# Storing and broadcasting the forgetting gates' sums from GpSimd's DMA queue instead of SyncE's

## The chip, the cores and the metric

The kernel runs on one core of one Trainium2 chip. The metric is the device time of one execution in microseconds (us), as the median of the runs; lower is better. The core's engines are named as in the profile: PE is TensorE, the matrix engine, with PEld for its weight loads; DVE is VectorE; ACT is ScalarE; POOL is GpSimd; SP is SyncE, which only issues transfers here. DMAs are issued from an engine's queue and carried out by 16 transfer engines.

## The reference

A trunk of two layers over 256 tokens of width 1024, in float32. Layer 0 mixes by forgetting attention (12 heads of 64), layer 1 by block-sparse attention with ALiBi; each also has 4 heads of attention into 256 memory tokens, and each is followed by a SwiGLU network. What the change touches is the forgetting gate of layer 0:

```
log_f = log_sigmoid(f_logit + b_fgate)          # per token and head
F = cumsum(log_f, axis=-1)                      # (heads, tokens)
s = q @ k.T * scale + F[..., :, None] - F[..., None, :]
p = softmax(where(causal, s, NEG));  out = p @ v
```

So every head needs F along the queries, one value per row of the scores, and F along the keys, one value per column, the same in all rows.

## The kernel before, in words

All matrix products are made in split precision: each float32 operand is cut into a high part (ACT, a copy that rounds, `hi`, line 204) and a low part (DVE, a subtraction, `lo`, line 205), and three products are summed in PSUM. Weights are laid out on the host as one stream of units of up to 2048 elements per partition (8 KB on each of 128 partitions, 1 MB in all). `fetch` (line 178) loads one unit into one of four `raw` buffers, from SP's queue; `split` (line 195) cuts half a unit into `hi` and `lo`, of which there are seven buffers each. A unit's fetch must wait until the unit four before it is split. `weights` (line 211) runs the splitting five halves ahead of PE's use, and `split` runs the fetching three units ahead of that.

`mixer` (line 430) makes one layer's attention. It first makes the values and, in layer 0, the gate logits; from these `lf` (lines 450 to 460) is log_f with tokens on the partitions. Then come three groups of queries and keys (`qk_ps`), of two head pairs each. Ahead of the second group, in layer 0, stands `memory_heads` (line 507): `mem_kv` (line 312) makes the keys and values of the memory (`mk`, `mv`), with the inverse root of the memory's mean square `rs_mem`, taken by POOL (line 245) and spread over the columns by PE and ACT as `rsb_mem` (line 257); then the memory queries `qm` are made, scaled and split into `xqm` (lines 351 to 353), and the keys into `mks` (lines 358 to 361). In these splits ACT makes the high parts, and POOL and DVE one low part each.

The attention of a pair of heads is a generator (`attend`, line 363) that is advanced by `step` between the products, so that its parts stand between other work. Among these generators is `gate_sums` (line 472). It makes the running sums F on PE as a product with a triangular matrix, with heads on 12 partitions; DVE copies them to `fr` (line 478); a DMA stores `fr` to the DRAM tile `fd` (line 479), and three DMAs read `fd` back, four heads each, broadcast to all 128 partitions of `fk` (line 482). F along the queries, `fq`, is made on PE and ACT directly. `bias` (line 489) joins `fk`, `fq` and the causal mask on DVE, head pair by head pair, and overwrites `fk`; the scores read the result (line 385).

The order of PE's and SP's instructions is that of the program's text (`manual_schedule`, line 713). The order on DVE, ACT and POOL is chosen by the compiler's scheduler, which may move an instruction ahead of others when its operands allow. Each engine then runs its own list strictly in order: an instruction that waits holds all that stand behind it, and the same is true of the DMAs in an engine's queue.

Of the kernel before, what the change touches and what calls it, by code (L numbers as in the profile page):

```python
# [28 lines left out]
P = 128  # L29
D = 1024  # L30
S = 256
NT = S // P
KD = D // P
H = 12
# [18 lines left out]
GATE_PARTS = 3  # L53
# [74 lines left out]
def trunk(ctx: ExitStack, tc: tile.TileContext, plan, stream, x, gains, norm_final, b_fgate, square, out):  # L128
    nc = tc.nc
# [27 lines left out]
    def bank(name):  # L157
        return Bank(pp.tile([P, 512], F32, tag="bank", name=name))
# [135 lines left out]
    fd = dp.tile([H, S], F32, name="fd")  # L294
    fk = cp.tile([P, H, S], F32, name="fk")
# [134 lines left out]
    def mixer(i, xs, rs):  # L430
# [41 lines left out]
        def gate_sums():  # L472
            yield
            fb = bank("F_ps")
            fb.mm(fb.t[:H, 0:S], lf[:, 0], prefix)
            fb.mm(fb.t[:H, P:S], lf[:, 1], prefix[:, 0:P], stop=True)
            fr = ap.tile([P, 2, S], F32, tag="work", name="fr", bufs=WORK_BUFS)[:H, 0]
            nc.vector.tensor_copy(fr, fb.t[:H, :S])
            nc.sync.dma_start(fd, fr)
            for g in range(GATE_PARTS):  # L480
                hs = slice(g * (H // GATE_PARTS), (g + 1) * (H // GATE_PARTS))
                nc.sync.dma_start(fk[:, hs], fd[hs].unsqueeze(0).to_broadcast([P, H // GATE_PARTS, S]))
            gb = bank("Fq_ps")
            for t in range(NT):
                for u in range(t + 1):
                    gb.mm(gb.t[:, t * H:(t + 1) * H], prefix[:, (t - u) * P:(t - u + 1) * P], lf[:, u], stop=u == t)
            nc.scalar.activation(fq.rearrange("p t h -> p (t h)"), gb.t[:, :NT * H], AF.Copy)
# [43 lines left out]
        for g in range(3):  # L531
            if g == MEM_AT[i]:
                memory_heads()
            kb = [bank(f"qk_ps{i}{2 * g + a}") for a in range(2)]
            for k in range(KD):
                wh, wl = weights(U["qk", i, g][k // 4], k % 4)
                for a in range(2):
                    for s in range(2):
                        c = slice(a * P, (a + 1) * P)
                        prod(kb[a], kb[a].t[:, s * S:(s + 1) * S], (wh[:, s, c], wl[:, s, c]),  # L540
                             (xs[0][:, k, :], xs[1][:, k, :]), k == KD - 1)
                if k % 2:
                    step()
            if g == 0:
                rsb = spread(rs, f"x{i}", (DH ** -0.5, 1.0), "x")
                if i == 0:
                    active.append(gate_sums())
            for a in range(2):
                p = 2 * g + a
                qk = ap.tile([P, 2, S], F32, tag="work", name=f"qk{i}{p}", bufs=WORK_BUFS)  # L550
                nc.vector.tensor_mul(qk.rearrange("p a s -> p (a s)"), kb[a].t, rsb.rearrange("p a s -> p (a s)"))
                xq = ap.tile([P, 2, S], F32R, tag="work", name=f"xq{i}{p}", bufs=WORK_BUFS)
                xk = ap.tile([P, 2, 2 * S], F32R, tag="pair", name=f"xk{i}{p}", bufs=PAIR_BUFS)
                no_lo(xk)
                split_queries(xq, qk[:, 0])
                split_keys(xk, qk[:, 1])
                idle = a + IDLE[i][g]
                active.append(attend(f"s{i}{p}", xq, xk, vsb, 2 * p, idle, bias, hT, p))
# [203 lines left out]
```

## Time and profile before

| what | value |
|---|---|
| median of 3 runs (lowest to highest) | 628.83 us (628.81 to 631.61) |
| the profiled execution's own time | 632.32 us |
| its span, first to last instruction | 630.5 us |
| busy, share of the span: PE, PEld, DVE, ACT, POOL | 97%, 83%, 63%, 58%, 10% |
| moved by DMA | 112.27 MB, mean 178 GB/s |
| PE's share of the chain of waits that ended last | 83% |

All stretches and durations come from the profiled execution; its time lies 3.5 us above the median of the runs. Times in the rows are us from the start of the span. In a timeline a row is the start, the duration, the engine, the line of the kernel, the operation, output<-input by the program's names, and in brackets the idle time of the engine ahead of it with what ended it; a q behind an engine's name is its sequencer or queue. For a DMA the duration is that of the issue, not of the transfer. The chain of waits is followed back from the last instruction through what released each step.

### The profile page before, as it was taken

How to read it: one execution, taken by the hardware profiler on the slowest of the kernel's cores; microseconds unless marked ns; L12 is line 12 of the kernel's file. 1: busy time of each engine (PE TensorE's matmuls, PEld its weight loads, DVE VectorE, ACT ScalarE, POOL GpSimd, SP SyncE). 2: the span in 40 equal slices, each digit the busy share in tenths (PEclk: the TensorE clock that was granted, in tenths of full speed). 3: DMA queues.
4: the chain of work that ended last, by engine and by line, in shares of the span. 5: the costliest groups of instructions: out<-in, count | busy, mean ns of one | idle time of the engine just before them, and what ended most of it. 6: DMA issues, size and time to landing. Idle time of an engine off the chain costs nothing.

```text
span 630.5 us, 8923 instructions
## 1 busy us (share of the span) xinstructions
PE 611.7 (97%) x3364; PEld 525.4 (83%) x3364; DVE 400.2 (63%) x696; ACT 363.0 (58%) x648; POOL 62.3 (10%) x91
## 2 busy tenths in 40 slices
PE   7999899999999999999999999999999999999994
PEld 5999887778888888888899999877888888888884
DVE  5678899976455544457475689986654455544535
ACT  6778877666444444446376589866644444444432
POOL 2021344300000000000011032200000000000002
PEclk9999799999999999999999999999999999999999
DMA  8985822345555555555555642332455555455301
GB/s 297 385 283 177 329 72 96 144 158 200 201 194 173 176 191 201 182 174 202 193 185 199 218 147 106 133 135 94 157 189 196 193 180 169 193 200 201 134 1 67
DMA packets 17636, 112.27 MB, mean 178 GB/s; under 512 B 2221, under 2 KB 2873, under 8 KB 5433
## 3 DMA queue, kind: packets, MB, share of 16 engines
q1 hardware_dynamic: 17304, 111.49, 49.1%
q8 instruction: 26, 0.43, 0.3%
q10 hardware_dynamic: 288, 0.22, 0.1%
q14 instruction: 18, 0.14, 0.1%
HBM read 110.64 MB, written 1.06 MB: 177 GB/s over the span
## 4 chain that ended last, share of the span: by engine, by line
PE 83%; DVE 7%; ACT 5%; DMA 2%; issue 1%; POOL 0%; SPq 0%; POOLq 0%; ACTq 0%; DVEq 0%
PE gu L167 38%; PE d_acc L167 18%; PE qk_ps L167 8%; PE v_ps L167 5%; PE o_acc L167 5%; DMA raw<-in_stream 2%; DVE lo L205 2%; PE hT L628 2%; ACT hi L204 1%; PE s_s L167 1%; ACT p_s L395 1%; PE mv_ps L167 1%; PE qm_ps L167 1%; PE mk_ps L167 1%; PE s_m L167 1%
## 5 line engine op out<-in xcount | busy, mean ns | idle before, releaser
L205 DVE TENSOR_TENSOR lo<-raw,hi 128x1024 fp32r<-128x1024 f32 (+3 forms) x201 | 238.3, 1203 | 159.8 <-ACT hi L204 154.5
L204 ACT ACTIVATE hi<-raw 128x1024 fp32r<-128x1024 f32 (+3 forms) x201 | 204.8, 1037 | 165.6 <-PE gu L167 78.9
L167 PE MATMUL gu<-hi,xh_ffn 128*128 128x512 f32 x352 | 139.0, 395 | 0.0
L167 PE MATMUL gu<-lo,xh_ffn 128*128 128x512 f32 x352 | 137.3, 390 | 0.0
L167 PE MATMUL gu<-hi,xl_ffn 128*128 128x512 f32 x352 | 137.1, 390 | 0.0
L167 PE MATMUL d_acc<-hi,h 128*128 128x512 f32 x348 | 107.5, 390 | 0.0
L167 PEld LDWEIGHTS gu<-lo,xh_ffn 128*128 128x128 f32 x352 | 66.1, 188 | 13.9
L167 PEld LDWEIGHTS gu<-hi,xl_ffn 128*128 128x128 f32 x352 | 66.2, 188 | 13.2
L167 PEld LDWEIGHTS gu<-hi,xh_ffn 128*128 128x128 f32 x352 | 66.1, 188 | 13.1
L167 PEld LDWEIGHTS d_acc<-hi,h 128*128 128x128 f32 x348 | 65.2, 188 | 13.8 <-DVE h L224 0.4
L167 PE MATMUL d_acc<-lo,h 128*128 128x512 f32 x174 | 67.7, 389 | 0.0
L167 PE MATMUL qk_ps<-xh_x,hi 128*128 128x256 f32 x192 | 55.8, 291 | 0.0
L167 PE MATMUL qk_ps<-xh_x,lo 128*128 128x256 f32 x192 | 55.1, 287 | 0.0
L167 PE MATMUL qk_ps<-xl_x,hi 128*128 128x256 f32 x192 | 55.1, 287 | 0.0
L619 ACT ACTIVATE sg<-gu,rs_f 128x256 f32<-128x256 f32 x44 | 20.5, 466 | 40.0 <-PE gu L167 40.0
L167 PEld LDWEIGHTS qk_ps<-xh_x,hi 128*128 128x128 f32 x192 | 37.7, 197 | 0.8 <-issue 0.8
L167 PEld LDWEIGHTS d_acc<-lo,h 128*128 128x128 f32 x174 | 32.7, 188 | 6.7
L167 PEld LDWEIGHTS qk_ps<-xh_x,lo 128*128 128x128 f32 x192 | 37.8, 197 | 0.0
L167 PEld LDWEIGHTS qk_ps<-xl_x,hi 128*128 128x128 f32 x192 | 37.6, 196 | 0.0
L620 DVE TENSOR_TENSOR hh<-gu,sg 128x256 f32<-128x256 f32 x44 | 18.5, 421 | 27.0 <-ACT sg L619 27.0
L395 ACT ACTIVATE p_s<-p_s,nmax_s 128x128 f32<-128x128 f32 (+1 forms) x48 | 21.4, 447 | 12.9 <-DVE nmax_s L385 12.7
L303 POOL MEMSET xk<- 64x256 f32 x24 | 7.4, 310 | 206.1 <-PE d_acc L167 180.7
(158 smaller groups left out, 852.3 us busy)
## 6 DMA issues: line engine op xcount, KB each, us to landing
raw<-in_stream SPq DMA_DIRECT2D x95, 1024.0 KB, 4.8
raw<-in_stream SPq DMA_DIRECT2D x4, 768.0 KB, 4.4
raw<-in_stream SPq DMA_DIRECT2D x2, 780.0 KB, 8.6
fk<-fd SPq DMA_DIRECT2D x3, 512.0 KB, 5.2
raw<-in_stream SPq DMA_DIRECT2D x3, 390.0 KB, 6.0
h<-in_x SPq DMA_DIRECT2D x2, 512.0 KB, 7.4
raw<-in_stream SPq DMA_DIRECT2D x1, 512.0 KB, 7.3
gfin<-in_norm_final SPq DMA_DIRECT2D x1, 512.0 KB, 3.6
```

The source lines that it names most:

```text
L167: nc.tensor.matmul(o, lhsT, rhs, start=self.fresh, stop=stop, skip_group_check=True)
L204: nc.scalar.activation(hi[:, c0:c1], src[:, c0:c1], AF.Copy)
L205: nc.vector.tensor_sub(lo[:, c0:c1], src[:, c0:c1], hi[:, c0:c1].bitcast(F32))
L303: nc.gpsimd.memset(dst[HOME[1 - a], a, S:].bitcast(F32), 0.0)
L395: nc.scalar.activation(pr[:, a, c], src, AF.Exp, bias=nmax[:, a, j], scale=scale, accum_out=total[:, a, j])
L619: nc.scalar.activation(sg[:, t], b[t].t[:, :FC], AF.Silu, scale=rs[t])
L620: nc.vector.tensor_mul(hh[:, t], b[t].t[:, FC:], sg[:, t])
L628: nc.tensor.transpose(b.t[:, j * S + t * P:j * S + (t + 1) * P], hh[:, t, j * P:(j + 1) * P], ident)
```

## The change

The store of the gates' sums and the three broadcasts are issued from POOL's DMA queue; nothing else in the text is changed.

```diff
             fr = ap.tile([P, 2, S], F32, tag="work", name="fr", bufs=WORK_BUFS)[:H, 0]
             nc.vector.tensor_copy(fr, fb.t[:H, :S])
-            nc.sync.dma_start(fd, fr)
+            nc.gpsimd.dma_start(fd, fr)
             for g in range(GATE_PARTS):
                 hs = slice(g * (H // GATE_PARTS), (g + 1) * (H // GATE_PARTS))
-                nc.sync.dma_start(fk[:, hs], fd[hs].unsqueeze(0).to_broadcast([P, H // GATE_PARTS, S]))
+                nc.gpsimd.dma_start(fk[:, hs], fd[hs].unsqueeze(0).to_broadcast([P, H // GATE_PARTS, S]))
```

## Rows read from the trace of the kernel before

**Rows 1.** The page: PE's busy time, and PE's granted clock in 40 slices.

```profile
PE 611.7 (97%) x3364; PEld 525.4 (83%) x3364; DVE 400.2 (63%) x696; ACT 363.0 (58%) x648; POOL 62.3 (10%) x91
...
PEclk9999799999999999999999999999999999999999
```

**Rows 2.** PE's waits, longest in total: total us, times, longest.

```profile
PE s_m L167 <- POOL xqm L353: 2.9, 1, 2.9
```

**Rows 3.** Windows: busy us of PE, PEld, DVE, ACT, POOL; PEclk, DMA share, GB/s.

```profile
63.00:64.00 1.00, 0.00 (x0) 0.00 (x0) 0.56 (x2) 0.95 (x3) 0.22 (x1) 1.00 1.09 414
64.00:65.00 1.00, 0.00 (x0) 0.00 (x0) 0.84 (x3) 0.95 (x3) 0.69 (x1) 0.66 0.98 311
...
70.00:72.00 2.00, 2.00 (x14) 2.00 (x14) 0.31 (x2) 0.00 (x0) 0.00 (x0) 0.72 1.01 426
```

**Rows 4.** The chain of waits in order of time, from 48 to 70.

```profile
52.42 6.83 DMA raw<-in_stream
...
65.12 2.08 PE s_m L167 x8
```

**Rows 5.** ACT's timeline from 52 to 64.

```profile
52.30 0.46 ACT L342 ACTIVATE mv<-mv_ps,rs_mem 128x256 f32<-128x256 f32 x1
...
59.33 1.06 ACT L204 ACTIVATE hi<-raw 128x1024 fp32r<-128x1024 f32 x1 [2.15 <-DMA raw<-in_stream]
```

**Rows 6.** DVE's timeline from 44 to 66.

```profile
45.15 0.41 DVE L478 COPY fr<-F_ps 12x256 f32<-12x256 f32 x1
...
50.44 2.36 DVE L205 TENSOR_TENSOR lo<-raw,hi 128x1024 fp32r<-128x1024 f32 x2 [0.58 <-ACT hi L204]
...
58.28 0.68 DVE L338 TENSOR_TENSOR mk<-mk_ps,rsb_mem 128x512 f32<-128x512 f32 x1
...
60.42 1.23 DVE L205 TENSOR_TENSOR lo<-raw,hi 128x1024 fp32r<-128x1024 f32 x1 [0.86 <-ACT hi L204]
...
63.87 0.61 DVE L499 SCALAR_TENSOR_TENSOR bias<-fk,fq,sq 128x128 f32<-128x128 f32 x2
```

**Rows 7.** SP's queue, timeline from 48 to 62.6.

```profile
49.82 2.92 SPq L187 DMA_DIRECT2D raw<-in_stream  x2
52.80 0.43 SPq L479 DMA_DIRECT2D fd<-fr  x1
59.46 1.30 SPq L482 DMA_DIRECT2D fk<-fd  x3
60.85 1.83 SPq L187 DMA_DIRECT2D raw<-in_stream  x3
```

**Rows 8.** POOL's groups by shape: busy us, mean ns of one, idle before.

```profile
L494 POOL TENSOR_SCALAR fk<-sq 128x256 f32<-128x256 f32 x12 | 14.5, 1209 | 15.2 <-DVE nmax_s L385 8.0 <-issue 6.5 <-POOL xk L303 0.2
...
L303 POOL MEMSET xk<- 64x256 f32 x24 | 7.4, 310 | 206.1 <-PE d_acc L167 180.7 <-PE s_s L167 20.7 <-issue 4.1
```

**Rows 9.** POOL's timeline from 44 to 66.

```profile
45.09 0.73 POOL L361 TENSOR_TENSOR xk<-qk,xk 64x256 fp32r<-64x256 f32 x1
50.00 0.55 POOL L245 TENSOR_TENSOR rs_mem<-me_mem,minus_half 128x1 f32<-128x1 f32 x1 [4.18 <-DVE me_mem L243]
...
60.77 1.47 POOL L361 TENSOR_TENSOR mk<-mk,mk 64x256 fp32r<-64x256 f32 x1 [7.28 <-ACT mk L358]
62.51 0.71 POOL L361 TENSOR_TENSOR mk<-mk,mk 64x256 fp32r<-64x256 f32 x1 [0.26 <-ACT mk L358]
```

**Rows 10.** DMA issues by line: count, KB each, median us from issue to landing.

```profile
fk<-fd SPq DMA_DIRECT2D x3, 512.0 KB, 5.2
...
out<-o SPq DMA_DIRECT2D x1, 320.0 KB, 2.5
```

**Rows 11.** The same windows as in rows 3, earlier stretches.

```profile
48.00:50.00 2.00, 2.00 (x19) 2.00 (x18) 1.86 (x3) 2.00 (x5) 0.00 (x0) 1.00 0.00 0
50.00:52.00 2.00, 2.00 (x19) 2.00 (x18) 1.56 (x2) 2.00 (x3) 0.55 (x1) 1.00 0.51 135
...
57.00:59.00 2.00, 2.00 (x19) 2.00 (x18) 2.00 (x4) 0.18 (x1) 0.00 (x0) 1.00 0.05 21
```

## The prediction

> **What bounds the kernel now.** The page first: TensorE (PE) is busy for 97% of the span, and its granted clock is at full speed (2.4 GHz) in all slices but two near a tenth of the span [rows 1]. So the change can only matter where PE waits. The waits of PE come next: the longest one after the start-up is 2.9 us, for GpSimd's (POOL's) split of the memory queries `xqm` [rows 2]. The windows around it show what this stop costs beyond itself: PE is idle in 63 to 64, the clock is 1.00 there, 0.66 in 64 to 65 and 0.72 in 70 to 72, so it lay at its half level (1.2 GHz) from about 64.3 to 71.1 [rows 3]. PE works again from 65.12 [rows 4], so 6.0 us of its work ran at half speed, which lost some 3.0 us. At stake around this place are thus 2.9 + 3.0 = 5.9 us.
>
> The change's four transfers lie just ahead of it. The chain of waits, read back from 65.12, goes through ScalarE's (ACT's) key and query splits to a weight fetch that was issued at 52.42 and landed 6.83 us later, at 59.25 [rows 4]. I call it B, and the fetch issued before it at 49.82 I call A. ACT stood idle 2.15 us for B, because `hi` of B lies ahead of the key splits in its queue [rows 5]. The keys `mk` themselves were ready on VectorE (DVE) at 58.28 + 0.68 = 58.96 [rows 6], and ACT took them up after 59.33 + 1.06, at 60.3 to 60.4: the wait for B costs the chain 1.3 us. The landing of B is what the whole prediction turns on.
>
> **What is removed.** On SyncE's queue (SP) the store of `fd` waited behind A and B: its data `fr` were ready at 45.15 + 0.41 = 45.56 [rows 6], it was issued at 52.80, and the three broadcasts of `fk` only at 59.46, because SP stood for the landing of `fd`; three more weight fetches then followed from 60.85 [rows 7]. Four issues (0.43 + 1.30 = 1.73 us) and a wait of 6.2 us leave SP. I cost that at nothing: B is issued ahead of `fd` in either kernel, so it does not start earlier, and the fetches behind, which could start up to 8 us earlier, line up after B; the chain goes on through no other fetch up to 65.12 [rows 4], so none of those three was late. The first reader of `fk` on DVE, the bias at 63.87 [rows 6], is off the chain too.
>
> **What is added on POOL.** Four DMA issues and one wait. No row shows a DMA issued from POOL. Its price g lies between POOL's memset (0.31 us) and its costliest full-tile instruction (1.21 us) [rows 8], with more as a possibility for the upper end; I take 1.2, since descriptors for 128 rows are nearer to the full tile. POOL ends its last key split at 45.82 [rows 9], so `fd` is issued at 45.9 and handed over at 47.1. The quickest landing in the trace took 2.5 us from issue, some 2.1 of it behind the issue itself [rows 10]; the transfer engines are empty in 48 to 50 [rows 11]. So `fd` lands near 49.2. POOL waits for that (about 2 us), then issues the three broadcasts, 3 x 1.2 = 3.6 us, up to 52.8. Behind them in POOL's queue stands the square root `rs_mem`, which before ran at 50.00 for 0.55 us [rows 9]; it would end at 53.4, 2.8 us late. Who waits: ACT's `mv` at 52.30 [rows 5], which slips to 53.4, by 1.1 us. That is inside the 1.3 us by which `mk` was early, so it costs nothing as long as that cover stands.
>
> **What is moved on the transfer engines.** This is the term that I count. The broadcasts move 3 x 512 KB [rows 10]; at 426 GB/s, the rate of a full stretch [rows 3], that is 1.573 MB / 0.426 = 3.7 us. Before, they ran after B. Now their first data come at about 50.4, beside A and ahead of B's last row. In 50 to 52 the engines had a share of 0.51 [rows 11], so 0.98 us was free. If all of `fk` is served before B ends, B lands 3.7 - 1.0 = 2.7 us later. A row of `raw` is 8 KB on each partition and one of an `fk` part 4 KB; if the two queues take turns row by row, only 1.05 MB of `fk` goes ahead of A's and B's 2.1 MB, 2.5 - 1.0 = 1.5 us. I take the middle, **2.1 us**; the ends are 0 (nothing ahead of B) and 3.7 (none of it in free time). B then lands at 61.35, `hi` of B, the key splits, `xqm` and PE's restart all come 2.1 us later, and the half-clock stretch behind it is as long as before. POOL's 1.1 us on ACT hides in the longer wait.
>
> One thing about B I carry over without knowing that it recurs: in 57 to 59 the share is 0.05 [rows 11], about one of 16 engines, so a single engine finished B two microseconds after the others.
>
> The Trainium skill ("DMA: Bandwidth & Descriptors", Anatomy of one DMA) gives about 2.0 us of fixed cost to a DMA from GpSimd. By that estimate `fd` would land at 47.9, `fk` would use more of the empty stretch, and the sum would be about 630 us; no run here shows it.
>
> **Sum.** The profiled execution took 632.32 us for a span of 630.5; the median of the runs is 628.83, 3.5 lower. The difference of +2.1 us is set against the median: 628.8 + 2.1 = **630.9 us**.
>
> **Rivals.**
>
> *POOL becomes the path (slower).* If an issue from POOL takes longer than I took, `rs_mem` is what is late. It ends at 48.55 + 4g; of a delay of ACT's `mv` beyond 52.30 the first 1.3 us are hidden, the rest moves PE's restart, in place of the 2.1 and not on top of it. Over 3.1 us late is reached with g = 2.0 (`rs_mem` at 56.7). A reason for it: DVE's `lo` subtraction held a POOL split, which took 1.47 us from 60.77 beside a `lo` from 60.42 to 61.65, where the next one took 0.71 with none beside it [rows 6, 9]. The `lo` pair from 50.44 lasts 2.36 us and falls on the broadcasts [rows 6]. Held once in full and with g at 1.5, `rs_mem` ends at 48.55 + 6.0 + 2.36 = 56.9: 4.6 - 1.3 = +3.3 us, **632.1**, and up to 634 if two are held. Against it: a DMA issue need not behave like a split that reads two tiles.
>
> The Trainium skill ("SBUF — State Buffer", SBUF: two separate sides) says that a DVE operation with two SBUF inputs locks out only a GpSimd operation that reads SBUF, while one in a 2-port mode keeps GpSimd from writing descriptors. By that rule `lo` would hold the splits, as the rows show, but not the issues, and the sum would stay at 630.9; by the hold of the rows it is 632.1 or more.
>
> *The wait for B goes away (faster).* If the engine that finished B late was late through the neighbourhood of `fd`, or if the compiler's new order on ACT puts the key splits ahead of `hi` of B, the key splits start at 58.96: 1.3 us earlier, and PE restarts at 63.8. The clock was still 1.00 in the window 63 to 64 [rows 3], so the half-speed stretch and its 3.0 us could go as well: 628.8 - 4.3 = **624.5**. Against it: `fk` must then not delay B, though it is moved towards it.
>
> *Nothing is seen.* `fk` is generated late or slowly enough to run after B, and POOL stays within its 1.3 us: **628.8**.
>
> *The order is not what the text of the kernel says.* Only PE's and SP's orders are fixed by hand. If `rs_mem` is put ahead of the broadcasts on POOL, its delay vanishes and the broadcasts start at about 53.5; B is still in transit, so 1 to 2 us remain: **630**.
>
> **How the numbers follow.** My forecast (B late by contention) gets 0.47, its own range 628.8 to 632.5; 0.05 of it lies over the bound. POOL as the path 0.22, the wait for B gone 0.16, nothing seen 0.10, other order 0.05. A measurement of this kernel tells about 0.5% (3.1 us) from no change: faster 0.16; slower 0.22 + 0.05 = 0.27; within it 0.57. The range reaches from the faster rival, 624.5, to 633.2, inside the slower one; what lies beyond (half of the faster case, under half of the slower) is 0.18.
>
> **What would show it.** Right: the `fd` store on POOL before 47, `fk` issued between 49 and 53, B's landing at 61 to 62, ACT's idle time before `hi` of B near 4 us, PE's wait for `xqm` near 5 us, one half-clock stretch as before. Wrong: B landing at or before 59.3; PE's wait named for `rsb_mem` or for `mv` instead; ACT taking the key splits before `hi` of B; PE's clock at full speed throughout; or another PE wait of microseconds elsewhere, which would mean that the order of ACT, DVE or POOL changed in a way that these rows cannot show.

## The result and the profile after

The changed kernel takes **633.43 us** (median of 8 runs, 632.70 to 634.26). The kernel before, run beside it, took 630.56 (8 runs, 628.81 to 631.61; the three runs shown ahead of the prediction are among them). The ratio is 1.0051 with a 95% interval of 1.0034 to 1.0068: 2.1 to 4.3 us slower. The forecast was 630.9 in a range of 624.5 to 633.2, so the time lies 0.2 us above its upper end.

PE's first page row is the same as before but for 0.2 us, and PE's waits show one change that matters. First the page's busy times and the clock of the changed kernel, then PE's longest wait after the start-up.

```profile
PE 611.9 (97%) x3364; PEld 525.6 (83%) x3364; DVE 399.9 (63%) x696; ACT 363.6 (57%) x648; POOL 65.0 (10%) x95
...
PEclk9999799999999999999999999999999999999998
```

```profile
PE s_m L167 <- POOL xqm L353: 5.7, 1, 5.7
```

The wait of [rows 2] has grown from 2.9 to 5.7 us. PE's busy time is equal to 0.2 us, so in these two executions the change is a matter of waiting alone. POOL has four instructions more, the four issues.

POOL's timeline (as in [rows 9]) shows what these cost there.

```profile
45.66 0.76 POOL L479 DMA_DIRECT2D fd<-fr  x1
48.37 1.62 POOL L482 DMA_DIRECT2D fk<-fd  x3 [1.96 <-DMA fd<-fr]
50.01 0.59 POOL L245 TENSOR_TENSOR rs_mem<-me_mem,minus_half 128x1 f32<-128x1 f32 x1
```

A store issue takes 0.76 us and a broadcast 0.54, against the 1.2 I took. All three broadcasts are issued before `rs_mem` is due, and `rs_mem` runs at 50.01, where it ran before (50.00). POOL delays nobody.

The chain of waits of the changed kernel, from 46 to 70, is the one to set against [rows 4].

```profile
47.23 2.10 DVE lo L205 x2
49.33 0.18 issue
49.51 0.11 DVE me_mem L243
49.62 9.11 DMA raw<-in_stream
58.76 0.04 issue
58.80 1.07 ACT hi L204
59.87 0.02 issue
59.90 1.25 DVE lo L205 x2
...
62.17 0.69 DVE mk L338
...
67.65 0.04 issue
67.69 2.07 PE s_m L167 x8
```

It does not go through B any more. The fetch in it was issued at 49.62: that is **A**, which landed 9.11 us later, at 58.73. Before, the same issue landed in 4.7 us, at 54.5, as the view of DMA issues of the kernel before, cut to 49 to 51, says (count, KB, us to landing):

```profile
raw<-in_stream SPq DMA_DIRECT2D x1, 1024.0 KB, 4.7
```

So A lost 4.2 us. ACT's timeline shows who stood for it (compare [rows 5]).

```profile
53.99 0.82 ACT L342 ACTIVATE mv<-mv_ps,rs_mem 128x256 f32<-128x256 f32 x2
58.80 2.01 ACT L204 ACTIVATE hi<-raw 128x1024 fp32r<-128x1024 f32 x2 [3.99 <-DMA raw<-in_stream]
60.72 0.36 ACT L256 ACTIVATE rsb_mem<-rsb_ps_mem 128x256 f32<-128x256 f32 x1
61.29 1.06 ACT L204 ACTIVATE hi<-raw 128x1024 fp32r<-128x1024 f32 x1 [0.21 <-DMA raw<-in_stream]
62.89 0.42 ACT L358 ACTIVATE mk<-mk 64x256 fp32r<-64x256 f32 x1 [0.54 <-DVE mk L338]
```

ACT is idle 3.99 us for A and only 0.21 us for B. The broadcast scale `rsb_mem` stands behind `hi` of A in ACT's list, and `mk` needs `rsb_mem`; on DVE `mk` also stands behind the two `lo` of A (59.90 to 62.17). So `mk` was made at 62.17 instead of 58.28 [rows 6], 3.9 us late; 1.3 us of this had been slack in which ACT stood for B, and PE's restart moved by 67.69 - 65.12 = 2.6 us. B itself landed at 61.2 against 59.25, 2.0 us late.

The windows show the cause (columns as in [rows 3]; compare [rows 11]).

```profile
48.00:50.00 2.00, 2.00 (x19) 2.00 (x18) 1.65 (x3) 2.00 (x5) 1.62 (x3) 1.00 0.13 25
50.00:52.00 2.00, 2.00 (x19) 2.00 (x19) 1.76 (x2) 2.00 (x3) 0.59 (x1) 1.00 1.00 277
...
57.00:59.00 2.00, 2.00 (x19) 2.00 (x18) 0.00 (x0) 0.20 (x1) 0.00 (x0) 1.00 1.03 430
...
70.00:72.00 2.00, 2.00 (x11) 2.00 (x11) 1.92 (x4) 1.98 (x5) 0.00 (x0) 0.50 0.00 0
```

The transfer engines, empty from 57 to 59 before, are full from 50 to 66 now, and DVE does nothing from 57 to 59, where it was busy all the time before.

**Where the time stands in the whole.** The first `gu` product, which begins the SwiGLU network of layer 0, splits the span well. It starts at 134.28 in the profile of before and at 136.23 in that of after; the profiled executions took 632.32 and 634.26. What is left behind that point is 498.04 and 498.03 us. The whole difference lies ahead of the first `gu`.

These two executions differ by 1.9 us, the medians by 2.9: the profiled execution of before lies 1.8 us above its median, that of after 0.8 above its own. The mean granted clock, which is known of every run, tells more. Among this case's profiles a mean of 0.996 to 0.998 goes with no stretch at the half level, 0.993 to 0.995 with one of some 3.4 us, 0.990 to 0.992 with one of some 6.8 us; the two executions here, at 0.992 and 0.990, are both of the last kind. Of 79 further runs of the kernel before, 25 are of the first kind, with a median of 629.05 us, 49 of the second, with 630.67, and 4 of the third, with 632.03 (one, at 0.944, is left aside). Of the changed kernel's 8 runs 7 are of the third kind, with a median of 633.53, and one, 632.81, is of the second. So at like clock the changed kernel is 1.5 to 2.1 us slower, and by this estimate the rest of the 2.9 us, about 1, is that it nearly always has the longer stretch at the half level.

### The profile page after: what moved, and what is told of

It reads as the page before. It is cut to its first block, busy times and chain, and to the rows that moved or that the text cites. A ratio compares the mean times of both kernels' runs of the same rounds, so it can differ in the third digit from the quotient of the medians.

```text
span 632.5 us, 8922 instructions
## 1 busy us (share of the span) xinstructions
PE 611.9 (97%) x3364; PEld 525.6 (83%) x3364; DVE 399.9 (63%) x696; ACT 363.6 (57%) x648; POOL 65.0 (10%) x95
## 4 chain that ended last, share of the span: by engine, by line
PE 83%; DVE 7%; ACT 5%; DMA 2%; issue 1%; POOL 0%; SPq 0%; POOLq 0%; DVEq 0%; ACTq 0%
PE gu L167 38%; PE d_acc L167 18%; PE qk_ps L167 7%; PE v_ps L167 5%; PE o_acc L167 5%; DVE lo L205 2%; DMA raw<-in_stream 2%; PE hT L628 2%; ACT hi L204 1%; PE s_s L167 1%; ACT p_s L395 1%; PE mv_ps L167 1%; PE qm_ps L167 1%; PE mk_ps L167 1%; PE s_m L167 1%
## 5 line engine op out<-in xcount | busy, mean ns | idle before, releaser
L167 PE MATMUL qk_ps<-xh_x,lo 128*128 128x256 f32 x192 | 55.2, 287 | 0.0
```

The lines of the kernel that those rows point to most:

```text
L167: nc.tensor.matmul(o, lhsT, rhs, start=self.fresh, stop=stop, skip_group_check=True)
```

## The experiments

Four theories. **T1**: the broadcasts go ahead of A, and PE's wait for `xqm` is the cost. **T2**: the compiler's new order on DVE and ACT is the cost. **T3**: issuing on POOL is the cost. **T4** replaced T1 after the second set of runs: what ACT and DVE lose while they stand for A is the cost, and PE's wait is only where it shows. Intervals are for the ratio to the kernel before, run on the same chip (630.23, 630.41 and 630.60 us in the three sets).

**The store alone on POOL.**

```diff
-            nc.sync.dma_start(fd, fr)
+            nc.gpsimd.dma_start(fd, fr)
```

> The store of the gates' sums is issued by POOL, the three broadcasts stay on SP. SP's list then has the two weight fetches A and B first and the broadcasts right behind them, with the store long landed. Theory T1 (the broadcasts' 1.5 MB, put ahead of A and B on the transfer engines, delays the memory keys and so PE's restart): A lands by 54.5 and B by 59.3 as in the kernel before, PE's wait for xqm is 2.9 us or less, and the time is that of the kernel before (ratio 0.994 to 1.001). Rival T2 (the compiler's new order on ACT and DVE costs the time): this order differs from that of before too, so a loss of some microseconds is possible. Rival T3 (DMA issues on POOL are what costs): about a quarter of the loss, +0.8 us.

Measured: 629.83 us, ratio 0.9997 (0.9981 to 1.0012). In its profile A lands at 55.2 and B at 58.9. The three broadcasts are issued on SP right behind B (53.3 to 54.9), without SP standing for `fd`, and land at 60.6 to 63.1, in time for the first bias. PE's wait is 2.2 us and no stretch is at the half level. So this DMA costs nothing that is measured by being issued on POOL, and neither does it gain anything that SP no longer waits 6.2 us.

**All four on POOL, the broadcasts held back until `rsb_mem` exists** (a one-column copy from it into each part of `fk`).

```diff
+            yield from iter(lambda: len(rsb_mem), 1)
...
+                nc.gpsimd.tensor_copy(fk[:, hs.start, 0:1], rsb_mem[0][:, 0:1])
                 nc.gpsimd.dma_start(fk[:, hs], fd[hs].unsqueeze(0).to_broadcast([P, H // GATE_PARTS, S]))
```

> All four transfers on POOL as in the change, but each broadcast is held until the factors rsb_mem exist (a one-column copy of rsb_mem into fk on POOL stands ahead of each), so that its data come behind A and mostly behind B. T1: A lands as in the kernel before, PE's wait for xqm is 2 to 3.5 us, time ratio to before 0.995 to 1.002. T3 (issuing on POOL costs): the loss of the change stays, ratio 1.005. T2 (order): the lists on ACT and DVE are near those of before, so no loss either; this run tells T1 and T2 apart from T3 alone.

Measured: 631.79 us, ratio 1.0027 (1.0012 to 1.0041). A lands at 54.5, B at 57.1, and PE's wait for `xqm` is down to 1.5 us: the delay of A hangs on the broadcasts' time. But the broadcasts, issued from 58.6 on, came behind three weight fetches that SP had issued meanwhile, and landed at 68.3 to 70.8. DVE's first bias, at 63.87 before [rows 6], was late, and PE waited elsewhere. Both rows of PE's waits in this kernel:

```profile
PE qk_ps L167 <- ACT p_m L395: 1.9, 2, 1.2
PE s_m L167 <- POOL xqm L353: 1.5, 1, 1.5
```

**The kernel before, with the change's four transfers made in addition** (through a second DRAM tile, from POOL's queue).

```diff
+    fd2 = dp.tile([H, S], F32, name="fd2")
...
+            nc.gpsimd.dma_start(fd2, fr)
+            [nc.gpsimd.dma_start(fk[:, 4 * g:4 * g + 4], fd2[4 * g:4 * g + 4].unsqueeze(0).to_broadcast([P, 4, S])) for g in range(3)]
             nc.sync.dma_start(fd, fr)
```

> The kernel before, with the change's four transfers added on POOL (a store to a second DRAM tile and three broadcasts from it into fk), and the kernel's own store and broadcasts kept on SP behind them. The lists of PE, DVE and SP are those of the kernel before; ACT's differs in the place of one mv. T1: A lands 4 us late (58 to 59), PE's wait for xqm grows to 5 to 6 us, time +2.5 to +4 us against before (ratio 1.004 to 1.0065). T2 (the compiler's new order of DVE and ACT costs the time): no loss, ratio 1.000. T3: a loss, but with A landing as before.

Measured: 634.38 us, ratio 1.0071 (1.0050 to 1.0092). PE's, DVE's and SP's lists are those of the kernel before, and ACT's differs in one `mv`. Still ACT stands for A as in the changed kernel:

```profile
58.76 2.01 ACT L204 ACTIVATE hi<-raw 128x1024 fp32r<-128x1024 f32 x2 [3.70 <-DMA raw<-in_stream]
```

PE's wait is 5.4 us. T2 falls: the extra transfers suffice without the new order.

**Only the first of the three broadcasts**, in the changed kernel (the other eight heads' `fk` set to zero, so their scores lack the gates' sums along the keys). In a first try the zeros were written by POOL near the start; that moved the whole start by 1 us (PE's first wait 4.5 instead of 2.8), so its 631.40 us, ratio 1.0022 (1.0008 to 1.0036), tells little.

```diff
+    nc.gpsimd.memset(fk[:, H // GATE_PARTS:], 0.0)
...
-            for g in range(GATE_PARTS):
+            for g in range(1):
```

> The change with only the first of the three broadcasts; the part of fk for the other eight heads is filled with zeros once, on POOL near the start, so these heads lack the gates' term along the keys. A third of the bytes stands ahead of A and B, and the lists of ACT and DVE are nearly those of the change. T1: A lands about 1.4 us later than before instead of 4.2, PE's wait for xqm is 3 to 4 us, time 0 to +1 us against before (ratio 1.000 to 1.002). T2: the loss of the change stays, ratio 1.005.

With the zeros written by DVE (`nc.vector.memset`) the start is as before:

> The changed kernel with only the first of the three broadcasts; the other eight heads' fk is set to zero on DVE near the start instead of on POOL, and their scores lack the gates' sums along the keys, so it leaves a part of the computation out. T1: 0.5 MB instead of 1.5 MB goes ahead of A, so A lands a third of the way from its place in the kernel before (54.5) to that in the changed one (58.7), about 55.9; PE's wait for xqm is 3.5 to 4.2 us and the time 1 us above the kernel before, a ratio of 1.000 to 1.003. Rival (the cost is one of issuing or of the first DMA, not of bytes): A lands near 58.7 and the time is that of the changed kernel, 1.005.

Measured: 631.19 us, ratio 1.0010 (0.9995 to 1.0025). A lands at 55.7, PE's wait is 3.2 us.

```profile
55.77 2.01 ACT L204 ACTIVATE hi<-raw 128x1024 fp32r<-128x1024 f32 x2 [0.89 <-DMA raw<-in_stream]
```

A third of the bytes gives some three tenths of A's delay (1.2 of 4.2 us) and a fifth of the cost (0.0010 of 0.0051, with an interval from nothing to half). The delay goes with the bytes, not with the first DMA.

**The first memory scores one step later in PE's order**, in the kernel before, in the changed one, and with the store alone on POOL. PE then has some 54 more products to do ahead of the place where it stood.

```diff
-IDLE_MEM = (1, 1)
+IDLE_MEM = (2, 1)
```

> The kernel before, with the memory heads' scores of the first two pairs put one step (some 54 products, about 6.3 us of PE at full speed) later in PE's order. It is the partner of the next run. Every theory: PE no longer stands 2.9 us for xqm at its first memory score, so that stop and the half-speed stretch behind it go, unless the split weights that it now reaches earlier are late themselves: 624.5 to 629, a ratio of 0.991 to 0.998 to the kernel before, with A landing near 54.5 and B near 59.2 as there.

> The changed kernel with the same later step. T1 (the change costs time only because the broadcasts delay fetch A and with it xqm, for which PE stands): A still lands near 58.7 and xqm is still ready near 67.5, but PE has about 6.3 us of products ahead of its first memory score and hardly stands for it, so the distance to its partner shrinks from 3 us to under 1 us: 625 to 629.5. T1b (the late fetch A starves PE directly, whatever stands at the memory score): PE waits 1 to 3 us for the split weights of A instead, and 2 to 3 us to the partner stay. T3 (issuing four DMAs on POOL costs time elsewhere, in all of the kernel or at its ends): the distance stays near 3 us with no wait at either place.

> The later step with only the store of fd on POOL's queue and the broadcasts left on SP's. T1: nothing goes ahead of A (it lands near 54.5 to 55), so it is as fast as the partner without the change, within 0.8 us. T3, if a DMA issued on POOL has a fixed price: over 0.8 us slower than that partner, about a quarter to a half of what the full change costs.

Measured, in this order: 630.62 us, ratio 0.9992 (0.9977 to 1.0006); 634.23, ratio 1.0053 (1.0032 to 1.0073); 630.60, ratio 1.0006 (0.9990 to 1.0022). This is the run that felled T1. In the kernel before, the 2.9 us stop is gone altogether, with no clock below full speed from 50 to 100, and the median gains nothing that is measured (at most 1.5 us by the interval). In the changed one the distance to its partner stays at 634.23 - 630.62 = 3.6 us, though PE's wait for `xqm` is only 1.7 us. PE's waits of the changed kernel with the later scores:

```profile
PE qk_ps L167 <- ACT p_m L395: 2.4, 2, 1.6
PE s_m L167 <- POOL xqm L353: 1.7, 1, 1.7
PE pT_s L406 <- DVE nmax_s L385: 1.5, 1, 1.5
```

The stop has moved to the next places where PE needs ACT and DVE: these two are behind, and PE meets them sooner or later. The windows of the kernel before with the later scores show the same from the other side (its whole profile lies 1.8 us later: PE waited 1.8 us instead of 1.1 for its first `hi`, and its clock was at the half level from 8.9 to 12.3):

```profile
60.00:70.00 10.00, 10.00 (x86) 10.00 (x85) 8.61 (x18) 8.63 (x17) 4.35 (x6) 1.00 0.85 300
70.00:80.00 10.00, 9.35 (x76) 8.84 (x76) 10.00 (x43) 9.44 (x30) 4.95 (x6) 1.00 0.67 279
80.00:90.00 10.00, 8.16 (x64) 6.74 (x62) 9.78 (x17) 9.65 (x25) 4.03 (x4) 1.00 0.28 105
```

PE runs through 60 to 70, and then loses 2.5 us in 70 to 90, where DVE is busy for 19.8 of 20 us. From 45 us to the first `gu` PE is idle for 5.1 us in all, against 5.5 in the kernel before: without this stop it stands elsewhere. What this profile does save is the stretch at the half level behind the stop, which many executions of the kernel before do not have either. The store's issue on POOL costs nothing here too; for the broadcasts' issues T3 is settled by the next kernels.

**Five raw buffers instead of four** (one `hi` buffer given up for the room), in the kernel before, the changed one and the one with the store alone on POOL. Each fetch then carries the unit that was one later, so what the broadcasts delay is needed later.

```diff
-        raw = wp.tile([P, UNIT], F32, tag="raw", name=f"raw{i}", bufs=4)
+        raw = wp.tile([P, UNIT], F32, tag="raw", name=f"raw{i}", bufs=5)
...
-        hi = wp.tile([P, HALF], F32R, tag="hi", name=f"hi{i}_{k0}", bufs=7)
+        hi = wp.tile([P, HALF], F32R, tag="hi", name=f"hi{i}_{k0}", bufs=6)
...
-    AHEAD, FETCH = 5, 3
+    AHEAD, FETCH = 5, 4
...
```

> The kernel before with five raw buffers instead of four (paid for with one of the seven hi buffers), so that each weight fetch is issued one split unit earlier. Partner of the next two runs. What was fetch A is then issued near 47 instead of 49.8 and lands near 50, what was B is issued near 49.8 and lands near 54.5. Every theory: ACT no longer stands for either, PE's wait for xqm shrinks from 2.9 to 0.5 to 2.5 us, and the time is 627 to 631, a ratio of 0.995 to 1.001.

> The changed kernel with five raw buffers. T4 (the change costs what ACT and DVE lose while they stand for fetch A; PE's wait is only where that loss shows): A is issued ahead of the broadcasts and lands before 54, so ACT's idle time of 4.0 us before hi of A goes; the fetch behind it takes A's place behind the broadcasts and lands near 58.7, when ACT has work up to some 57 to 58, so ACT stands 1 to 2 us. The distance to the partner shrinks from 3.2 us to 0 to 1.5 us: 628 to 631.5. T3 (issuing on POOL, or any other cost that does not hang on A): the distance stays near 3 us, 630 to 634.

> Five raw buffers with only the store of fd on POOL's queue. T4: as fast as the partner without the change or up to 1 us faster, since fk lies behind the fetches and does not wait for fd: 626.5 to 630.5. T3: up to 1 us slower than the partner.

Measured, in this order: 634.44 us, ratio 1.0062 (1.0041 to 1.0084); 633.18, ratio 1.0046 (1.0031 to 1.0061); 632.78, ratio 1.0047 (1.0031 to 1.0063). All three are slower than expected: behind the first `gu` they take 500.3 to 500.4 us instead of 498.1, with new waits of PE there (`gu` for `xl_ffn`, 1.5 us), which is the price of this edit and not of the change. Among them the change costs nothing: its median is 1.3 us below its partner's. In the changed kernel with five buffers the fetch of 49.55 still lands only at 59.2, 9.7 us after its issue, but ACT has `hi` of the unit before it in hand:

```profile
54.63 2.24 ACT L204 ACTIVATE hi<-raw 128x1024 fp32r<-128x1024 f32 x2
56.78 0.36 ACT L256 ACTIVATE rsb_mem<-rsb_ps_mem 128x256 f32<-128x256 f32 x1
59.09 0.42 ACT L358 ACTIVATE mk<-mk 64x256 fp32r<-64x256 f32 x1 [1.94 <-DVE mk L338]
```

The transfer is as late as in the changed kernel, and nobody stands for it. That is T4. All four transfers are issued on POOL in this kernel, so T3 falls for the broadcasts too.

**The broadcasts alone on POOL**, the store left on SP.

```diff
-                nc.sync.dma_start(fk[:, hs], fd[hs].unsqueeze(0).to_broadcast([P, H // GATE_PARTS, S]))
+                nc.gpsimd.dma_start(fk[:, hs], fd[hs].unsqueeze(0).to_broadcast([P, H // GATE_PARTS, S]))
```

> The other half of the change alone: the store of fd stays on SP's queue behind A and B, the three broadcasts go to POOL's. T4: fd lands near 59.4 as in the kernel before, so POOL issues fk at 59.5 to 61 and A (54.5) and B (59.2) are not delayed; POOL's split of mk, at 60.77 before, slips by some 0.3 us: a ratio of 0.998 to 1.002. T3 (three broadcasts issued on POOL cost time of themselves): 1.003 to 1.006.

Measured: 635.93 us, ratio 1.0096 (1.0067 to 1.0125), the slowest of all. The time is above both expectations. POOL issued the broadcasts from 58.57 to 60.4, where I expected them, but they landed only at 67.8 to 70.6. On SP they had kept the later weight fetches behind them; off SP, three fetches of 1 MB went ahead (52.9, 55.7, 58.0). DVE's timeline shows what hung on it:

```profile
62.16 0.42 DVE L361 TENSOR_TENSOR mk<-mk,mk 64x256 fp32r<-64x256 f32 x1 [0.70 <-ACT mk L358]
67.80 0.35 DVE L499 SCALAR_TENSOR_TENSOR bias<-fk,fq,sq 128x128 f32<-128x128 f32 x1 [5.22 <-DMA fk<-fd]
68.18 0.42 DVE L353 TENSOR_TENSOR xqm<-qm,xqm 64x256 fp32r<-64x256 f32 x1
```

In this kernel's order a `bias` stands ahead of a split of `xqm` on DVE, so PE waits for `xqm` again, by way of `fk`. It is a loss of the order on the transfer engines, not of issuing on POOL.

**The profiles side by side.** "PE waits" are those for `xqm` and, behind a plus, the largest other of 0.5 us or more from 60 to 90. "PE idle" is PE's idle time from 45 us to the first `gu`; "half level" is what the lower clock costs PE ahead of the first `gu`, half of its busy time in the stretches in which windows of 0.5 us show the half level. DVE's busy time is that of the window 50 to 100. The first try with one part, whose start differs, is left out.

| kernel | PE waits | PE idle | half level | DVE busy, 50 to 100 | first `gu` | profiled time | time behind first `gu` |
|---|---|---|---|---|---|---|---|
| before | 2.9 | 5.5 | 3.0 | 43.86 | 134.28 | 632.32 | 498.0 |
| changed | 5.7 | 7.3 | 3.1 | 41.68 | 136.23 | 634.26 | 498.0 |
| store alone | 2.2 | 4.5 | 0 | 47.56 | 131.29 | 629.46 | 498.2 |
| broadcasts held back | 1.5 + 1.9 | 6.1 | 3.1 | 42.43 | 135.57 | 633.73 | 498.2 |
| done twice | 5.4 | 7.9 | 1.6 | 42.54 | 135.57 | 633.95 | 498.4 |
| one part (zeros by DVE) | 3.2 | 4.9 | 1.6 | 45.21 | 132.74 | 630.83 | 498.1 |
| before, later scores | none + 1.8 | 5.1 | 1.7 (ahead of 45) | 46.83 | 133.78 | 631.85 | 498.1 |
| changed, later scores | 1.7 + 2.4 | 7.8 | 1.7 | 42.68 | 136.04 | 634.07 | 498.0 |
| store alone, later scores | none + 1.8 | 4.4 | 1.7 | 47.26 | 132.53 | 630.66 | 498.1 |
| broadcasts alone | 6.2 | 8.9 | 3.8 | 41.92 | 137.87 | 635.96 | 498.1 |
| before, five buffers | 1.6 + 1.8 | 5.9 | 1.7 | 42.66 | 133.95 | 634.29 | 500.3 |
| changed, five buffers | 1.9 + 0.8 | 5.6 | 0 | 45.01 | 131.97 | 632.37 | 500.4 |
| store alone, five buffers | 1.6 + 1.6 | 5.9 | 0 | 44.58 | 132.53 | 632.94 | 500.4 |

Each row is one execution, and not always near its kernel's median: "broadcasts held back" lies 1.9 us above its own. PE's work ahead of the first `gu` is the same in all rows, so its idle time and the half level account for the differences: without them, and without PE's 3.1 to 4.6 us of idle time ahead of 45, 121.9 to 123.2 us are left in every row. From "before" to "changed" the idle time grows by 1.8 us and what the half level costs by less than 0.1. With the later scores the change adds 2.7 us of idle time, though the wait for `xqm` is short; with five buffers it adds none.

The time follows the first `gu`, and the first `gu` follows what DVE has got done by 100 much better than it follows PE's wait for `xqm`: "before" waits 2.9 us and "changed, later scores" 1.7, and the second is the later one by 1.8 us. This is a correlation, and "before, five buffers" is an exception (less done than in "before", and an earlier first `gu`). Two of the rows in the form of the windows, of the kernel before and of the changed one:

```profile
50.00:100.00 50.00, 46.41 (x359) 43.62 (x358) 43.86 (x109) 39.65 (x93) 18.52 (x22) 0.93 0.54 201
```

```profile
50.00:100.00 50.00, 44.35 (x345) 42.21 (x344) 41.68 (x103) 38.46 (x91) 18.23 (x22) 0.93 0.53 199
```

DVE has done 2.2 us less by 100 and ACT 1.2 us less; the first `gu` is 1.95 us later.

## Why the prediction was right in part, and where it failed

*Right.* The direction; the cause (1.5 MB of broadcasts put ahead of weight fetches); the size of B's delay, 2.0 us against 2.1 taken; PE's wait, "near 5 us" against 5.7; and the half-level stretch behind it. The difference, 2.1 us against a ratio that says 2.1 to 4.3, is right at its lower end, and in part by luck: PE's restart moved by 2.6 us and by another path than the one that I priced. One of the signs did not come: ACT's idle time before `hi` of B was 0.21 us and not "near 4 us"; the 3.99 us stood ahead of `hi` of A.

*The step that failed: "B lands at 61.35, `hi` of B, the key splits, `xqm` and PE's restart all come 2.1 us later".* I defined A and B, and let the broadcasts fall "beside A and ahead of B's last row", but priced only B, since the chain of before went through B. The broadcasts were issued from 48.37 on, 1.3 us ahead of A; the transfer engines begin at 49.6, where I had the first data at 50.4, and A lost 4.2 us, twice what B lost. For A the sum had nothing. With A at 58.7, `hi` of A, `rsb_mem` and two `lo` are late, and they lie ahead of `mk` on ACT and DVE. The chain of after runs through A, where that of [rows 4] ran through B. The trace of before could have told: A landed at 54.5, ACT took up `hi` of A without having stood for it and then worked without a gap up to 57.2, so A had 0.4 us of slack, and a delay of it passes to ACT and DVE alike. ACT's timeline of the kernel before:

```profile
54.55 0.46 ACT L342 ACTIVATE mv<-mv_ps,rs_mem 128x256 f32<-128x256 f32 x1
54.91 2.00 ACT L204 ACTIVATE hi<-raw 128x1024 fp32r<-128x1024 f32 x2
56.80 0.38 ACT L256 ACTIVATE rsb_mem<-rsb_ps_mem 128x256 f32<-128x256 f32 x1
```

*Why they were issued so early: POOL's price.* I took 1.2 us for an issue; the runs show 0.76 and 0.54. The broadcasts were handed over by 50.0 and not by 52.8. The row nearest in kind was not the full-tile instruction of 1.21 us but a value just above the memset's 0.31, the lower end that I named.

*What was at stake was misjudged.* I wrote "at stake around this place are thus 2.9 + 3.0 = 5.9 us" and priced the rival without the wait for B at 624.5. The kernel before with later scores took the stop away, and the half-level stretch behind it, and won nothing that is measured (0.9992, 0.9977 to 1.0006); PE's idle time up to the first `gu` fell by 0.3 us and not by 2.9. PE's stop was a place where PE waited for two engines that were behind in this stage; without the stop it waits further on. The 3.0 us at the half level were lost in the profiled execution, but 25 of 79 later runs of the same kernel had no such stretch, and their median, 629.05, is no more than 1.6 us below that of the 49 with the shorter one. With the store alone on POOL there was no half-level stretch in the profile either, and the median is unchanged. So the faster rival was worth little, and most of the range below 628 was there for no reason.

*The base.* This term of the sum was mis-sized by more than the difference was. The sum was set on 628.83, the median of three runs of which two lay near 628.8. Later runs put the kernel before at 630.2 to 630.6. Of the 2.5 us between 630.9 and 633.43, 1.7 is this base (630.56 - 628.83), the other 0.8 the difference itself. A reading of the base's page was off too, with nothing resting on it: its clock row [rows 1] has one slice below 9, the fifth, and not two.

*The other rivals.* POOL as the path: no, `rs_mem` ran at its old time. A different order on POOL: no, the broadcasts stand ahead of `rs_mem`, as in the text. Nothing seen: no. The three issues of 1.62 us ran beside a `lo` pair (47.2 to 49.6) without being held, where a POOL split beside a `lo` took 1.47 us [rows 9]. By the Trainium skill ("SBUF — State Buffer", SBUF: two separate sides) a two-input DVE operation locks out only a GpSimd operation that reads SBUF; the trace agrees, 0.54 us each.

The Trainium skill's fixed cost of about 2.0 us for a DMA from GpSimd ("DMA: Bandwidth & Descriptors", Anatomy of one DMA) put `fd`'s landing at 47.9. It landed at 48.1, 2.4 us after the start of its issue, so the trace nearly agrees; the sum of 630 that I drew from it was wrong for the same reason as mine, that it looked at B alone.

*Left open.* The 1.5 to 2.1 us at like clock rest on few runs (7 against 4, and 1 against 49). Why the changed kernel nearly always has the longer stretch at the half level was not tested; that its stop of PE is longer is only a guess at the reason. A kernel with the key splits put ahead of `hi` of A on ACT was not tried. No kernel tried here beats the one before.

## What to carry to other kernels

A transfer that is moved to another queue gets a new place among all transfers: it goes ahead of what it stood behind, and loses what it kept behind it. Look for the next reader of every transfer that it now goes ahead of, not only of the one in the chain; the chain of before names one late transfer and says nothing of one that was just in time. And where PE waits in a stage in which another engine is busy nine tenths of the time, the length of that wait is not what a change there can win or lose: sum PE's idle time over the whole stage, and what the other engine gets done.

## What the runs showed of the hardware that was not expected

- A DMA issue takes POOL 0.76 us for the store of 12 rows of 1 KB, and, in the changed kernel, 0.53 to 0.58 us for each broadcast into 128 rows of 4 KB; SP's issues of the same broadcasts took 1.30 / 3 = 0.43 us [rows 7].
- 512 KB issued on POOL with three fetches of 1 MB outstanding landed 9 to 11 us later (58.57 to 67.8 and 59.9 to 70.6 in the run with the broadcasts alone on POOL). The median is 5.2 us in the kernel before [rows 10], and also in the changed kernel, where the broadcasts went ahead of the fetches.
- Of two transfers of 1 MB behind the broadcasts, the earlier lost 4.2 us and the later 2.0. That fits the time from 57 to 59, which had been empty and is full now.
